# First loads of a decoder layer cut differently: activations in halves of 64 rows on both queues, first weights in three loads, four short warm-up products instead of seven

## The chip, the cores and the metric

The kernel runs on one core of one Trainium2 chip. The metric is device time in microseconds of one execution, the median of several. Profiles are single executions; their times count from the first instruction of the span.

TensorE multiplies matrices, VectorE and ScalarE work element by element, GpSimd does small side work. Transfers from main memory are issued on the queue of SyncE (SP) or of ScalarE (ACT), here called SP's queue and ScalarE's queue, and some on GpSimd's.

## The reference

One inference step of one decoder layer on 320 tokens: 256 of a prompt and 8 sequences of 8 sample tokens, with shared weights, model width 2048, all in 32-bit floats. Cut to what matters here:

```python
xn = rms_norm(x, g_mix)                      # x: 320 x 2048
z  = xn @ w_in                               # B, C, h, q, k, v and two gates
u  = c_gate * h_conv                         # short causal convolution, width 3
y_conv = (b_gate * short_conv(u)) @ w_conv_out
y_attn = window_attention(q, k, v, rel_bias, sinks) @ w_attn_out
h  = x + (sigmoid(gate_c) * y_conv + sigmoid(gate_a) * y_attn) @ w_o
hn = rms_norm(h, g_ffn)
h  = h + (silu(hn @ w_gate) * (hn @ w_up)) @ w_down
y  = rms_norm(h, g_final)
```

It returns the normalised output of both groups and the new key, value and convolution states.

## The kernel before

**Precision and layout.** Activations lie with features on the 128 partitions and the 320 tokens along the row: 16 chunks of 128 features. Each 32-bit factor is split into a high part, rounded to TensorE's 32-bit matmul type, and a low part, the remainder. A product of chunk k then takes three matmuls for each 128 output columns: high x times high w, low x times high w, high x times low w. For weights ScalarE makes the high part (`whi`) and VectorE the low part (`wlo`); for activations likewise (`xh_t`, `xl_t`), in `x_prep`, where for chunk 0 VectorE makes both. The norm's factor per token is applied later, so products can start on x times `g_mix`.

**Order of work.** The program is one long sequence of weight-driven products: first k and v (`kv_product`), then q, C, H, B, the gates, the attention between them, `w_o`, and the feed-forward part. Weights stream through four buffers of 512 KB (`wraw`). The order in which each engine takes its instructions comes from a scheduler of the language's layer: it places instructions by its own estimates, and adds the waits. A load that has to be counted takes one of eight counters in turn; when all eight are taken, the next load waits on its queue until the load that had that counter eight loads before has landed.

**The start.** This is all that the change touches.

- `xv` holds all activations and the small vectors. `x_load(i)` loads a stretch of its columns for all 128 partitions: `x_load(0)` the 16 columns of `g_mix` and chunk 0 (336 columns, 168 KB, line 290), `x_load(1)` chunk 1 (160 KB, on ScalarE's queue, line 294), later ones one or two chunks.
- `first_w` is the buffer of the weights of chunk 0 and chunk 1 for k and v, each 512 columns wide. Chunk 0 of it is loaded in two halves of 256 columns (128 KB each), the first on ScalarE's queue (line 292), the second on SP's (line 293). Chunk 1 (256 KB) follows on SP's queue from `load_kv` (line 331).
- ScalarE then loads its function table with a tiny square root (line 329), rounds chunk 0 in blocks of 128, 128 and 256 columns (line 337), and goes on chunk by chunk (line 129).
- While these loads are under way TensorE multiplies a constant by itself (lines 302 to 305): 15 warm-up products of 256 columns and 7 of 128, on bf16 ones that need no load. Their result is not used.
- `kv_product` (line 346, matmuls on line 372) runs over the 16 chunks, as tiles of 1, 1, 1, 1, 2, 2, 2, 2, 2, 2, with four blocks of 128 output columns: 12 matmuls of 320 columns a chunk. For chunk 0 the twelve are sorted by kind: four high-high, four with low x, four with low w.

Of the kernel before, what the change touches and what calls it, by code (L numbers as in the profile page):

```python
# [17 lines left out]
T = TP + NB * TS  # L18
# [8 lines left out]
P = 128  # L27
KC = D // P
CW = 256
# [7 lines left out]
VW = 16  # L37
# [15 lines left out]
def hybrid_layer(ctx: ExitStack, tc: tile.TileContext, a: dict, o: list):  # L53
    nc = tc.nc
    y_0, y_r, nk_p, nv_p, nk_s, nv_s, ncv = o

    w_in, w_kv, w_co, w_ao, w_o, w_g, w_u, w_d = (
        a[n] for n in ("w_in", "w_kv", "w_conv_out", "w_attn_out", "w_o", "w_gate", "w_up", "w_down")
    )
# [202 lines left out]
    xv = xp.tile([P, VX + 56], F32, name="xv")  # L262
# [23 lines left out]
    def x_load(i, eng=nc.sync):  # L286
        c0, c1 = (VW + sum(XB[:j]) * T if 0 < j < len(XB) else j and VX + 56 for j in (i, i + 1))
        return eng.dma_start(xv[:, c0:c1], a["x_v"][:, c0:c1])

    x_load(0)  # L290
    first_w = wp.tile([P, KT // 2, 2 * DKV], F32, tag="wraw", name="first_w", bufs=4)
    nc.scalar.dma_start(first_w[:, 0, 0:CW], w_kv[0, :, 0, 0:CW])
    nc.sync.dma_start(first_w[:, 0, CW:], w_kv[0, :, 0, CW:])
    behind = x_load(1, nc.scalar)
    first_root = st.tile([P, 1], F32, name="first_root")
# [5 lines left out]

    wm = ps_aux("wm")
    one = lambda n: nc.const_aps.tensor(1.0, [P, n], mybir.dt.bfloat16)
    for n in [CW] * 15 + [P] * 7:
        nc.tensor.matmul(wm[:, :n], one(P), one(n), start=True, stop=True)

    def x_prep(kc):
# [517 lines left out]
    for cp in range(4):  # L825
# [8 lines left out]
        for c in range(2):  # L834
# [13 lines left out]
            n = UL - 2  # L848
# [475 lines left out]
```

## Time and profile before

| | us |
|---|---|
| median of 3 runs | 1593.41 (1593.38 to 1593.64) |
| the profiled execution, its own time | 1593.85 |
| its span, first to last instruction | 1592.1 |
| TensorE busy in the span | 1583.2 |
| VectorE busy | 890.9 |
| ScalarE busy | 645.9 |
| first product of k and v starts | 4.43 |
| first product of chunk 1 starts | 7.20 |

The profile is read from its stages: a table that gives, for a stretch of the span, the busy time of each engine, the granted clock, the share of the 16 transfer engines in use and the rate in GB/s. The chain of waits goes back from the end to what released each step. In the timeline's rows the first two numbers are the start and the length in us; "idle before" in square brackets says how long the engine had stood still and what released it. PEld is TensorE's weight load, beside the matmuls. SPq and ACTq are instructions that issue transfers; their length is that of the issue, and the time to landing stands in the list of loads.

### The profile page before, as it was taken

The page shows a single profiled execution, that of the slowest core. Times are in us where ns is not written, and L with a number is a line of the kernel's source. Part 1 is how long each engine was busy: PE and PEld are TensorE (multiplying, and loading weights), DVE is VectorE, ACT ScalarE, POOL GpSimd, SP SyncE. Part 2 cuts the span into 40 slices and gives each one's busy share as a digit, 9 for nine tenths or more (in the row PEclk, how much of TensorE's full clock was granted, in tenths as well). Part 3 has the DMA queues.
Part 4 walks back from the last instruction along what each step waited for, and adds up shares of the span by engine and source line. Part 5 has one row for each costly group of instructions (what it writes and reads, how often), then busy time and mean ns, then how long its engine had stood idle before and what let it go on. Part 6 is the DMA issues. An engine that isn't in the chain of part 4 may idle for free.

```text
span 1592.1 us, 26453 instructions
## 1 busy us (share of the span) xinstructions
PE 1583.2 (99%) x10899; PEld 1547.1 (97%) x10899; DVE 890.9 (56%) x1314; ACT 645.9 (41%) x917; POOL 133.2 (8%) x213
## 2 busy tenths in 40 slices
PE   9999999999999999999999999999999999999998
PEld 9999999999999999999999999998888999999887
DVE  7879765445555445556555555553444455555556
ACT  7554443333333333344333333333333334444443
POOL 1414332000000003320000000000000000000021
PEclk9999999999999999999999999999999999999999
DMA  7757566544455544455554545555555454445663
GB/s 271 207 182 218 171 211 203 166 154 155 157 159 159 159 156 155 155 158 159 157 154 155 159 158 159 159 156 161 155 155 157 157 159 158 156 155 157 190 180 131
DMA packets 77648, 266.06 MB, mean 167 GB/s; under 512 B 9832, under 2 KB 13112, under 8 KB 77400
## 3 DMA queue, kind: packets, MB, share of 16 engines
q1 hardware_dynamic: 71736, 249.99, 50.2%
q0 software_dynamic: 5360, 13.84, 3.0%
q8 instruction: 85, 1.39, 0.4%
q10 hardware_dynamic: 432, 0.56, 0.1%
q14 instruction: 35, 0.29, 0.1%
HBM read 257.27 MB, written 9.04 MB: 167 GB/s over the span
## 4 chain that ended last, share of the span: by engine, by line
PE 99%; DMA 0%; DVE 0%; ACT 0%; issue 0%; SPq 0%; DVEq 0%
PE fu L186 19%; PE fg L186 19%; PE dn L997 9%; PE wo L186 7%; PE gc L186 7%; PE ga L186 7%; PE dn L1005 6%; PE C L186 3%; PE B L186 3%; PE H L186 3%; PE q L186 3%; PE ya L186 3%; PE yc L186 3%; PE dl L1001 2%; PE kv L372 2%; PE dn L1162 1%
## 5 line engine op out<-in xcount | busy, mean ns | idle before, releaser
L130 DVE TENSOR_TENSOR wlo<-wraw,whi 128x1024 fp32r<-128x1024 f32 (+1 forms) x460 | 563.1, 1225 | 564.5 <-ACT whi L129 453.4
L129 ACT ACTIVATE whi<-wraw 128x1024 fp32r<-128x1024 f32 (+1 forms) x460 | 485.5, 1056 | 722.0 <-PE fu L186 129.5
L186 PE MATMUL fu<-hh_t,whi 128*128 128x320 f32 x704 | 205.0, 301 | 0.0
L186 PE MATMUL fu<-hl_t,whi 128*128 128x320 f32 x704 | 205.0, 301 | 0.0
L186 PE MATMUL fg<-hh_t,whi 128*128 128x320 f32 x704 | 205.0, 301 | 0.0
L186 PE MATMUL fg<-hl_t,whi 128*128 128x320 f32 x704 | 205.0, 301 | 0.0
L186 PE MATMUL fu<-hh_t,wlo 128*128 128x320 f32 x704 | 158.8, 301 | 0.0
L186 PE MATMUL fg<-hh_t,wlo 128*128 128x320 f32 x704 | 158.8, 301 | 0.0
L997 PE MATMUL dn<-a_t,whi 128*128 128x512 f32 x640 | 155.2, 382 | 0.0
L186 PEld LDWEIGHTS fu<-hh_t,whi 128*128 128x128 f32 x704 | 131.7, 187 | 0.0
L186 PEld LDWEIGHTS fu<-hl_t,whi 128*128 128x128 f32 x704 | 131.7, 187 | 0.0
L186 PEld LDWEIGHTS fg<-hh_t,whi 128*128 128x128 f32 x704 | 131.7, 187 | 0.0
L186 PEld LDWEIGHTS fg<-hl_t,whi 128*128 128x128 f32 x704 | 131.7, 187 | 0.0
L997 PEld LDWEIGHTS dn<-a_t,whi 128*128 128x128 f32 x640 | 115.4, 187 | 16.5 <-issue 1.2
L186 PEld LDWEIGHTS fg<-hh_t,wlo 128*128 128x128 f32 x704 | 116.1, 187 | 0.0
L186 PEld LDWEIGHTS fu<-hh_t,wlo 128*128 128x128 f32 x704 | 116.1, 187 | 0.0
L1005 PEld LDWEIGHTS dn<-a_t,wlo 128*128 128x128 f32 x640 | 97.7, 188 | 6.9
L1005 PE MATMUL dn<-a_t,wlo 128*128 128x320 f32 x640 | 103.4, 301 | 0.0
L186 PE MATMUL gc<-xh_t,whi 128*128 128x320 f32 x256 | 74.5, 301 | 0.0
L186 PE MATMUL gc<-xl_t,whi 128*128 128x320 f32 x256 | 74.5, 301 | 0.0
L186 PE MATMUL ga<-xh_t,whi 128*128 128x320 f32 x256 | 74.5, 301 | 0.0
L186 PE MATMUL ga<-xl_t,whi 128*128 128x320 f32 x256 | 74.5, 301 | 0.0
(317 smaller groups left out, 2695.7 us busy)
## 6 DMA issues: line engine op xcount, KB each, us to landing
wraw<-in_w_in_dram SPq DMA_DIRECT2D x128, 512.0 KB, 3.9
wraw<-in_w_gate_dram SPq DMA_DIRECT2D x88, 512.0 KB, 3.8
wraw<-in_w_up_dram SPq DMA_DIRECT2D x88, 512.0 KB, 3.7
wraw<-in_w_down_dram SPq DMA_DIRECT2D x88, 512.0 KB, 3.7
wraw<-in_w_o_dram SPq DMA_DIRECT2D x32, 512.0 KB, 3.8
wraw<-in_w_conv_out_dram SPq DMA_DIRECT2D x16, 512.0 KB, 3.6
wraw<-in_w_attn_out_dram SPq DMA_DIRECT2D x16, 512.0 KB, 3.7
wraw<-in_w_kv_dram SPq DMA_DIRECT2D x6, 512.0 KB, 7.5
```

The source lines that it names most:

```text
L129: last["hi"] = nc.scalar.activation(hi, src, AF.Copy)
L130: last["lo"] = nc.vector.tensor_sub(lo, src, hi.bitcast(F32))
L186: last["mm"] = nc.tensor.matmul(turns(fives(ps[c][:, :T])), w[:, k, c * P:(c + 1) * P], turns(x(kc)), start=(kc == 0 and i == 0), stop=(kc ...
L372: last["mm"] = nc.tensor.matmul(turns(fives(ps[c][:, :T])), w[:, k, c * P:(c + 1) * P], turns(x(kc)), start=(kc == 0 and m == 0), stop=(kc ...
L997: nc.tensor.matmul(turns(placed(ps[c])), parts[k][0][:, cs], turns(a_move(k)), start=k == 0, stop=False)
L1001: nc.tensor.matmul(low, a_low(k), parts[k][0], start=k == 0, stop=k == nf - 1 and c0 < E0)
L1005: last["mm"] = nc.tensor.matmul(turns(placed(ps[c])[:, :, 0:JT]), parts[k][1][:, cs], turns(a_move(k)[:, :, 0:JT]), start=False, stop=k == ...
L1162: nc.tensor.matmul(turns(placed(ps[c])[:, :, JR:]), held[k][0][:, cs], turns(a_move(k)[:, :, JR:]), start=k == 0, stop=k == nf - 1,)
```

## The change

Three edits at the start of the program, and nothing else:

- `x_load(0)` becomes two loads of the same 336 columns: partitions 0 to 63 on SP's queue, 64 to 127 on ScalarE's.
- Chunk 0 of the first weights is loaded in three pieces: columns 0 to 127 on ScalarE's queue, 128 to 255 and 256 to 511 on SP's.
- The warm-up products of 128 columns are four, where they were seven.

```diff
-    x_load(0)
+    for rows, eng in ((slice(0, 64), nc.sync), (slice(64, P), nc.scalar)):
+        eng.dma_start(xv[rows, :VW + T], a["x_v"][rows, :VW + T])
     first_w = wp.tile([P, KT // 2, 2 * DKV], F32, tag="wraw", name="first_w", bufs=4)
-    nc.scalar.dma_start(first_w[:, 0, 0:CW], w_kv[0, :, 0, 0:CW])
+    nc.scalar.dma_start(first_w[:, 0, 0:P], w_kv[0, :, 0, 0:P])
+    nc.sync.dma_start(first_w[:, 0, P:CW], w_kv[0, :, 0, P:CW])
     nc.sync.dma_start(first_w[:, 0, CW:], w_kv[0, :, 0, CW:])
     behind = x_load(1, nc.scalar)
...
-    for n in [CW] * 15 + [P] * 7:
+    for n in [CW] * 15 + [P] * 4:
         nc.tensor.matmul(wm[:, :n], one(P), one(n), start=True, stop=True)
```

On SP's queue the program began, before the change, with these loads (a name in front of the arrow is where the load goes, behind it the source, then partitions x columns; `DMAHW0` and so on are the counters that a load waits for):

```order
L288 DMA xv<-in_x_v_dram 128x336
L293 DMA first_w<-in_w_kv_dram 128x256
L331 DMA first_w<-in_w_kv_dram 128x512
L288 DMA xv<-in_x_v_dram 128x320
L331 DMA wraw_191<-in_w_kv_dram 128x512
L288 DMA xv<-in_x_v_dram 128x320
L331 DMA wraw_191<-in_w_kv_dram 128x512 [waits DMAHW0_49]
L288 DMA xv<-in_x_v_dram 128x640 [waits DMAHW1_49]
```

With the change SP's queue begins so:

```order
L291 DMA xv<-in_x_v_dram 64x336
L294 DMA first_w<-in_w_kv_dram 128x128
L295 DMA first_w<-in_w_kv_dram 128x256
L333 DMA first_w<-in_w_kv_dram 128x512
L288 DMA xv<-in_x_v_dram 128x320
L333 DMA wraw_190<-in_w_kv_dram 128x512 [waits DMAHW0_49]
L288 DMA xv<-in_x_v_dram 128x320 [waits DMAHW1_49]
L333 DMA wraw_190<-in_w_kv_dram 128x512 [waits DMAHW2_49]
```

The load of weight chunk 1 (L331, now L333, 128x512 into `first_w`) moved from the third to the fourth place. The loads of weight chunk 2 and activation chunk 3, which waited for nothing, now wait for counters 0 and 1, which the two halves of the first activations hold.

On TensorE, the end of the warm-up products and the products of chunk 0, before:

```order
L305 MATMUL wm<-const-bfloat16-1.0 128x128
L372 MATMUL kv_143<-xh_t,whi_150 128x16x5x4 [waits DVE_49,Activation_49]
L372 MATMUL kv_144<-xh_t,whi_150 128x16x5x4 [waits Activation_49]
L372 MATMUL kv_145<-xh_t,whi_150 128x16x5x4 [waits Activation_49]
L372 MATMUL kv_146<-xh_t,whi_150 128x16x5x4
L372 MATMUL kv_143<-xl_t,whi_150 128x16x5x4 [waits DVE_49]
L372 MATMUL kv_144<-xl_t,whi_150 128x16x5x4
```

and with the change:

```order
L307 MATMUL wm<-const-bfloat16-1.0 128x128
L374 MATMUL kv_142<-xh_t,whi_149 128x16x5x4 [waits DVE_49,Activation_49]
L374 MATMUL kv_143<-xh_t,whi_149 128x16x5x4 [waits Activation_49]
L374 MATMUL kv_142<-xl_t,whi_149 128x16x5x4 [waits DVE_49]
L374 MATMUL kv_144<-xh_t,whi_149 128x16x5x4 [waits Activation_49]
L374 MATMUL kv_145<-xh_t,whi_149 128x16x5x4
L374 MATMUL kv_143<-xl_t,whi_149 128x16x5x4
```

The first product with the low activations (`xl_t`) moved from the fifth to the third place. ScalarE's queue issues three loads where it issued two: the second half of the first activations, the first 128 columns of weights, and activation chunk 1. Behind these places the order of instructions on every engine is the same in both programs.

## The prediction

> **What bounds the kernel now.** I read the page first, for the share of the engines.
>
> ```profile
> span 1592.1 us, 26453 instructions
> PE 1583.2 (99%) x10899; PEld 1547.1 (97%) x10899; DVE 890.9 (56%) x1314; ACT 645.9 (41%) x917; POOL 133.2 (8%) x213
> PE 99%; DMA 0%; DVE 0%; ACT 0%; issue 0%; SPq 0%; DVEq 0%
> ```
>
> TensorE is busy 1583.2 of 1592.1 us, so 8.9 us of the span are left for anything else. The table of stages (busy time and, behind it, the clock, the DMA share and the rate) tells where they lie.
>
> ```profile
> core 0: us, PE busy (x) PEld busy (x) DVE busy (x) ACT busy (x) POOL busy (x), PEclk, DMA share, GB/s
> 1.50:2.50 1.00, 1.00 (x7) 0.67 (x6) 0.00 (x0) 0.78 (x1) 0.78 (x3) 1.00 0.51 57
> 2.50:4.44 1.94, 1.82 (x16) 1.36 (x14) 0.66 (x2) 1.21 (x4) 0.00 (x0) 1.00 1.06 376
> 4.44:6.49 2.05, 2.05 (x12) 1.68 (x12) 1.59 (x3) 0.88 (x3) 0.00 (x0) 1.00 1.06 348
> 7.20:16.00 8.80, 8.80 (x62) 8.80 (x63) 8.57 (x16) 8.71 (x19) 2.70 (x6) 1.00 1.02 393
> 16.00:1584.80 1568.80, 1568.76 (x10806) 1534.08 (x10804) 877.44 (x1287) 631.98 (x888) 127.81 (x198) 1.00 0.53 165
> 1584.80:1592.10 7.30, 0.00 (x0) 0.00 (x0) 2.22 (x6) 1.71 (x4) 1.06 (x1) 0.67 0.60 229
> ```
>
> From 7.20 to 1584.8 us TensorE does not stop: 8.80 of 8.80 and 1568.76 of 1568.80. The tail of 7.3 us behind it contains no TensorE work. So whatever an edit does in the first microseconds reaches the end only by moving the moment 7.20, from which the unbroken run starts. The chain of waits over the first 10 us says what sets that moment (start, length, what):
>
> ```profile
> 0.80 0.39 SPq L288
> 1.24 0.42 SPq L293
> 1.70 4.79 DMA first_w<-in_w_kv_dram
> 6.52 0.64 ACT whi L129
> 7.20 2.83 PE kv L372 x18
> ```
>
> It is not the first activations and not the first weight chunk. It is the load of weight chunk 1 (I call it k1), third on SP's queue, issued at 1.70 and landed at 6.49; then ScalarE's rounding of it, 0.64 us, and TensorE at 7.20. Before that, TensorE has worked off chunk 0:
>
> ```profile
> 3.74 0.55 DVE L309 TENSOR_SCALAR xh_t<-xv 128x320 fp32r<-128x320 f32 x1 [2.42 <-DMA xv<-in_x_v_dram]
> 3.94 0.94 ACT L337 ACTIVATE whi<-first_w 128x128 fp32r<-128x128 f32 x3 [0.72 <-DMA first_w<-in_w_kv_dram]
> 4.43 1.05 PE L372 MATMUL kv<-xh_t,whi 128*128 128x320 f32 x4
> 5.32 0.72 PE L372 MATMUL kv<-xl_t,whi 128*128 128x320 f32 x4
> 5.88 0.72 PE L372 MATMUL kv<-xh_t,wlo 128*128 128x320 f32 x4
> 7.20 0.42 PE L372 MATMUL kv<-xh_t,whi 128*128 128x320 f32 x1 [0.60 <-ACT whi L129]
> ```
>
> Its twelve products start between 4.43 and 6.30. Those of a full-rate group are (0.72 - 0.30) / 3 = 0.14 us apart (0.30 is what one takes), so the thirteenth could start at 6.44; it starts at 7.20. This 0.76 us is all that chunk 0's timing has to spare, and all that an earlier k1 alone could give.
>
> **Is k1 late because the transfers are saturated?** Ahead of and with k1 lie 168 + 128 + 128 + 160 + 256 = 840 KB, 0.86 MB (the sizes are in the next rows: first activations, first weights in two parts, second activations on ScalarE's queue, k1). By the table of stages 57 + 1.94 x 376 + 2.05 x 348 = 1500 KB (in thousands of bytes) had moved by 6.49; 0.86 MB had moved by about 4.65. So 0.64 MB of later transfers moved before k1's last piece came in, and that last piece is about 1.8 us behind the mean rate. A load counts as landed when its last part has landed; one laggard among the parts decides here, not the order of issue.
>
> **The change part by part.** The issue rows (start, length) and the time to landing of the same loads:
>
> ```profile
> 0.79 0.41 ACTq L292 DMA_DIRECT2D first_w<-in_w_kv_dram  x1
> 1.24 0.45 ACTq L288 DMA_DIRECT2D xv<-in_x_v_dram  x1
> 1.72 1.28 ACT L329 ACT_TABLE_LOAD   x1 [1.72 <-PEq L1304]
> 2.66 0.43 SPq L331 DMA_DIRECT2D wraw<-in_w_kv_dram  x1
> 3.93 0.33 SPq L331 DMA_DIRECT2D wraw<-in_w_kv_dram  x1
> 6.51 0.33 SPq L331 DMA_DIRECT2D wraw<-in_w_kv_dram  x1
> 7.87 0.62 ACT L129 ACTIVATE whi<-wraw 128x512 fp32r<-128x512 f32 x1
> wraw<-in_w_kv_dram SPq DMA_DIRECT2D x2, 256.0 KB, 4.8
> first_w<-in_w_kv_dram SPq DMA_DIRECT2D x1, 256.0 KB, 4.8
> xv<-in_x_v_dram SPq DMA_DIRECT2D x1, 168.0 KB, 2.9
> first_w<-in_w_kv_dram ACTq DMA_DIRECT2D x1, 128.0 KB, 3.1
> first_w<-in_w_kv_dram SPq DMA_DIRECT2D x1, 128.0 KB, 3.2
> xv<-in_x_v_dram ACTq DMA_DIRECT2D x1, 160.0 KB, 3.4
> ```
>
> *Activations in halves.* The first 168 KB become 84 KB on each queue, at 0.80 and 0.79. Both must land before VectorE's L309 can start. If each half took half of the 2.9 us that lie between issue and landing, it would land 1.45 us earlier; but the stage 1.50:2.50 shows 57 GB/s against 376 in the next, with the same queues filled: the start of motion costs most of it. From 2.50 on, 168 KB at 376 GB/s take 0.46 us, and before they shared that rate with 128 KB of weights, 0.81 us together; so between nothing and 0.35 us earlier, and I take 0.2: the halves are joined by 128 KB of weights right behind, as before.
>
> The Trainium skill, page "DMA: Bandwidth & Descriptors", section "Rules for kernel authors", says of two transfers to disjoint partition halves that one need not bother, as both spread over the same engines. By that rule this term would be 0, by the rows 0.2 us earlier; the DMA share of 1.06 with two queues filled agrees that they share one capacity.
>
> *First weights in three loads.* The first block of 128 columns goes out second on ScalarE's queue, at about 1.24 instead of 0.79, the second block second on SP's. If 3.1 us to landing holds from the issue, the first block lands at 4.34 instead of 3.9, 0.44 later; if what counts is the bytes, 64 + 64 KB are in with the same bytes ahead and come at the old time. ScalarE also issues one load more ahead of its table load, which thus ends near 3.45 instead of 3.0 (1.72 + 1.28), still half a microsecond ahead of the weights at 3.94. I take +0.1 for the first product, at most +0.44, against the 0.2 us gained on the activations, which both must be there: the first product stands between 4.3 and 4.9. Even 4.9 puts the thirteenth at 6.9, still ahead of 7.20. That cover is the 0.76 us above; without it the worst case would cost those 0.44 us in full.
>
> *Everything behind on SP's queue.* Two loads more are counted in all, one of them on SP, so k1 goes out fourth on SP, one issue (1.70 - 1.24 = 0.46) later, at 2.16. Here lies the price that the trace can't settle. Two ends: loads of 256 KB took 4.8 us from issue to landing, the one issued at 1.70 and the two behind it alike; if that holds, k1 lands at 6.96 and the run starts 0.46 later. If the backlog holds, it costs nothing: the weights' third part landed at 1.24 + 3.2 = 4.44, so at 2.16 SP's transfers still had 2 us of other bytes ahead of k1, and the total is unchanged. The rate row of 376 GB/s with a share of 1.06 is nearer to the second: 0. On the other side, a new cut of the rows may hit no laggard; then k1 lands before 5.7 and the run starts at 6.44: -0.76. I take the middle of +0.46 and -0.76, -0.15.
>
> *The loads behind k1.* They now wait for a landing two loads further on: in the order of the change the third chunk's load waits on the first half of the activations. It went out at 2.66 with no wait; it goes out when that half has landed, 3.4 to 3.7, about 0.9 later. That it is a real wait is seen in the row at 3.93, which goes when the first weights landed (ScalarE starts on them at 3.94), and that at 6.51, right behind k1's landing at 6.49. What is queued behind it on SP is the next activations and the fourth chunk. The third chunk landed at 2.66 + 4.8 = 7.5 and is rounded at 7.87; TensorE wants it at 7.20 + 12 x 0.14 = 8.88, so with 0.62 us for the rounding the landing may slip to 8.2, that is by 0.7. A slip of 0.9 in full would cost 0.2; since bytes and not issues are the limit, I take 0.
>
> *Three warm-up products fewer, and one product moved.* Chunk 0's third product is now one on the low activations (ready at 4.87, 4.32 + 0.55, by the trace's next VectorE step), in place of one on the third weight block (ready at 3.94 + 0.94 = 4.88): 0.
>
> ```profile
> 0.83 2.72 PE L305 MATMUL wm<-const-bfloat16-1.0 128*128 128x256 bf16 x12 [0.83 <-PEq L1304]
> 3.52 0.80 PE L305 MATMUL wm<-const-bfloat16-1.0 128*128 128x256 bf16 x9
> 4.32 0.55 DVE L312 SCALAR_TENSOR_TENSOR xl_t<-xv,xh_t 128x320 fp32r<-128x320 f32 x1
> L305 PE MATMUL wm<-const-bfloat16-1.0 128*128 128x256 bf16 x15 | 3.1, 389 | 0.8 <-PEq L1304 0.8
> L305 PE MATMUL wm<-const-bfloat16-1.0 128*128 128x128 bf16 x7 | 0.6, 221 | 0.0
> ```
>
> The first 12 are (2.72 - 0.39) / 11 = 0.21 us apart, 1.2 columns a ns; the last nine, two wide and seven short, bring 1280 columns in 0.80 - 0.22 us, 2.2 a ns. So the clock rose at about 3.5 us, though the column of granted clock says 1.00 throughout. Three short ones at 2.2 columns a ns are 0.17 us: the warm-ups end at 4.15 instead of 4.32. The activations are ready at 3.74 + 0.55 = 4.29, so the warm-ups were hardly in the way; the gap ahead of the first product grows to about 0.3 us. Price on the end: 0.
>
> **The sum.** In the profiled execution: run start 7.20, minus 0.15, plus 1577.6 us of unbroken products and 7.3 us of tail: 1591.95 of span, and 1.75 around it (1593.85 measured against 1592.1), 1593.7. That execution lies 0.44 above the median of the runs; on the median, 1593.41 - 0.15 = 1593.3 us.
>
> **The rivals.**
>
> *A, the laggard goes.* k1 lands by 5.7, the run starts as soon as chunk 0 is done. For it: 0.64 MB overtook k1's last piece, which is no steady state. Against it: both other 256 KB loads took 4.8 us too. Price -0.76, up to -0.96 with the activations 0.2 earlier: 1592.5 to 1592.7. VectorE and ScalarE, at 8.57 and 8.71 of 8.80 us, leave little room to feed a faster run than that.
>
> *B, slower: issue counts.* k1 lands 4.8 us after its later issue: +0.46, 1593.9; if the third chunk slips too, 1594.1. For it the equal 4.8 us of three loads; against it the backlog. It decides from the point where k1 lands after 6.49.
>
> *C, the late clock.* The clock is raised later than at 3.5 us in other executions. The warm-ups then run at 0.21 and 0.105 us, seven short ones end at 0.83 + 3.15 + 0.74 = 4.7, four at 4.4; chunk 0 at half rate lasts 3.4 us, so TensorE and not k1 sets the run's start, and 0.3 us are saved: 1593.1. The trace holds one execution only, with the rise at 3.5. The Trainium skill, page "TensorE: Matmul & The Clock Gate", section "What you observe" and what follows it, has the window free-running and the count of slow products varying from run to run, which is this rival; no row here shows a second phase.
>
> *D, the clock falls back.* The longer gap of 0.3 us lets TensorE's clock stay or return to half. Chunk 0 then takes 1.68 us more, its end moves from 6.44 to 8.12, 0.92 past 7.20; each further chunk costs another 1.68. Against it: TensorE already stood still for 0.60 us ahead of 7.20, and the products after it keep the full rate. With chunk 0 and 1 slow: 1596.0.
>
> *E, nothing moves:* k1 and its laggard land as before; 1593.4. It is inside the forecast's own spread.
>
> **How the numbers follow.** Forecast with E, -0.4 to +0.3 around it: 0.60. A 0.15, B 0.18, C 0.04, D 0.03. What a measurement of this kernel can tell from no change is about 0.2%, 3.2 us. No case but a long D reaches it: even A is 0.06%. Faster by more: 0.01; slower by more: 0.02 (D, and small unknowns); within: 0.97. The range takes in A at its lower end (1592.4) and B at its upper with the 0.44 us by which one execution already differed from the others: 1592.4 to 1594.3.
>
> **What would show it.** In the changed kernel's chain the load of chunk 1 still stands ahead of the unbroken run, issued near 2.16, and TensorE's idle time ahead of it between 0 and 1 us. The first product starts at 4.3 to 4.9. The third chunk's load is issued after 3.3. The warm-ups end near 4.15, and from the second chunk on products are 0.14 us apart. I am wrong in the mechanism if TensorE stops anywhere after its second chunk, if the products of chunk 0 or 1 are 0.28 apart, or if the run starts before 6.2 or after 8.

## The result and the profile after

The changed kernel takes 1595.70 us (median of 22 runs, 1594.58 to 1597.05), the kernel before 1593.55 us (1592.95 to 1594.08). The ratio is 1.0013 with a 95% interval of 1.0007 to 1.0019: slower by 2.15 us. That lies inside 0.2% as forecast, but the interval is clear of 1, and the time is outside the predicted range of 1592.4 to 1594.3. Two runs at several thousand us, one of before here and one of e8 below, were disturbed and are left out of every range.

The profiled execution of the changed kernel took 1595.98 us with a span of 1594.2. Its table of stages, with the same columns as the one of before:

```profile
1.50:2.50 1.00, 1.00 (x7) 0.69 (x6) 0.00 (x0) 0.00 (x0) 0.77 (x3) 1.00 0.29 65
2.50:4.44 1.94, 1.94 (x12) 1.43 (x10) 0.70 (x2) 1.49 (x2) 0.00 (x0) 1.00 0.78 195
4.44:6.49 2.05, 1.24 (x6) 1.06 (x5) 0.97 (x2) 0.82 (x3) 0.00 (x0) 1.00 1.00 345
16.00:1584.80 1568.80, 1568.80 (x10811) 1534.79 (x10811) 878.39 (x1287) 633.54 (x892) 130.25 (x201) 1.00 0.53 165
1586.50:1594.20 7.70, 0.00 (x0) 0.00 (x0) 2.22 (x6) 1.70 (x4) 1.07 (x1) 0.71 0.58 218
```

The row from 16.00 us is as before: TensorE does not stop behind the start. The second row and the last are not.

Between 2.50 and 4.44 us the transfers moved 195 GB/s; before, in the same stage, 376. That is (376 - 195) x 1.94 = 350 KB less, close to 1 us of transfer at the old rate. By 2.50 us as much had moved as before (65 KB, 57 before), so the loss lies within this stage. The DMA share fell less than the rate, from 1.06 to 0.78: the transfer engines stood still more, and also moved less while they were busy (195 / 0.78 = 250 GB/s against 376 / 1.06 = 355).

The last row is the tail, from TensorE's last product to the end. It takes 7.7 us where it took 7.3. Both kernels end with SyncE waiting on the eight transfer counters, one after the other in a fixed order. The change counts two loads more, so every later transfer has a counter two further on. Before, the last output write had the counter that is asked last but one; now it has the one that is asked first, and seven waits of about 0.06 us each follow behind its landing. SyncE's waits for the output, first before, then with the change (us in total, times, longest):

```profile
SPq L1312 <- DMA out_dram<-ya: 1.8, 3, 0.8
SPq L1314 <- DMA out_dram<-ya: 2.3, 1, 2.3
```

That write lands 6.4 us behind TensorE's last product in both. All seven profiles with two loads more (the change, its two repeats, e1, e5, e7 and e8 below) have a tail of 7.75 to 7.77 us, the seven others one of 7.28 to 7.36. So about 0.43 us of the loss arise at the end of the program and have nothing to do with late data or the clock. No experiment was made for this path alone; the profiles show it.

The chain of waits over the first 10 us:

```profile
0.80 0.58 ACTq L291
1.42 3.63 DMA first_w<-in_w_kv_dram
5.07 0.32 ACT whi L339
5.43 4.68 PE kv L374 x18
```

It now runs through the first weight block, second on ScalarE's queue, and no longer through weight chunk 1. The rows of the timeline behind it:

```profile
0.80 0.58 SPq L291 DMA_DIRECT2D xv<-in_x_v_dram  x1
0.83 3.79 PE L307 MATMUL wm<-const-bfloat16-1.0 128*128 128x256 bf16 x19 [0.83 <-PEq L1306]
1.42 0.86 ACTq L293 DMA_DIRECT2D first_w<-in_w_kv_dram  x1
1.44 0.56 SPq L294 DMA_DIRECT2D first_w<-in_w_kv_dram  x1
5.43 0.90 PE L374 MATMUL kv<-xh_t,whi 128*128 128x320 f32 x2 [0.81 <-ACT whi L339]
7.32 0.61 ACT L129 ACTIVATE whi<-first_w 128x512 fp32r<-128x512 f32 x1
7.73 1.27 PE L374 MATMUL kv<-xh_t,wlo 128*128 128x320 f32 x4
8.79 0.47 PE L374 MATMUL kv<-xh_t,whi 128*128 128x320 f32 x1
9.33 0.36 PE L374 MATMUL kv<-xh_t,whi 128*128 128x320 f32 x1
9.52 0.31 PE L374 MATMUL kv<-xl_t,whi 128*128 128x320 f32 x1
9.67 0.30 PE L374 MATMUL kv<-xh_t,whi 128*128 128x320 f32 x1
```

Two things are to be seen. The loads of 64 rows were issued in 0.58 us, where 128 rows had taken 0.39; the load behind on ScalarE's queue took 0.86 us to issue (0.41 before), and landed at 1.42 + 3.63 = 5.05. So the first product starts at 5.43, 1.0 us later than before, after TensorE has stood still for 0.81 us. And its clock is still low: four products of chunk 0 take 1.27 us, (1.27 - 0.47) / 3 = 0.27 us apart, and the spacing falls to 0.14 only at about 9.4 us. Before, that fall came near 3.5 us, in the warm-up products.

Chunk 1 starts at 8.79, at 7.20 before. Its weights were rounded by 7.93 (the row at 7.32: ScalarE came to them late, behind the second activations, which landed at 2.31 + 4.4 = 6.7 where they had landed at 1.24 + 3.4 = 4.6). With a raised clock chunk 1 could so have started at about 8.0, an estimate; a2 below does at 8.03. Of the 1.59 us some 0.8 are then late data and 0.8 the low clock. The 1.59 us, 0.11 in the run of products behind it and 0.43 in the tail are together the 2.13 us between the two profiled executions.

### The profile page after: what moved, and what is told of

It is laid out like the page before. It is cut to its first block, busy times and chain, and to the rows that moved or that the text cites. A ratio compares the mean times of both kernels' runs of the same rounds, so it can differ in the third digit from the quotient of the medians.

```text
span 1594.2 us, 26451 instructions
## 1 busy us (share of the span) xinstructions
PE 1584.8 (99%) x10896; PEld 1549.0 (97%) x10896; DVE 891.7 (56%) x1314; ACT 645.8 (41%) x917; POOL 134.0 (8%) x213
## 4 chain that ended last, share of the span: by engine, by line
PE 99%; DMA 0%; DVE 0%; ACT 0%; issue 0%; DVEq 0%; ACTq 0%
PE fu L186 19%; PE fg L186 19%; PE dn L999 9%; PE wo L186 7%; PE ga L186 7%; PE gc L186 7%; PE dn L1007 6%; PE C L186 3%; PE B L186 3%; PE H L186 3%; PE q L186 3%; PE ya L186 3%; PE yc L186 3%; PE dl L1003 2%; PE kv L374 2%; PE dn L1164 1%
## 5 line engine op out<-in xcount | busy, mean ns | idle before, releaser
L186 PE MATMUL wo<-m_h,whi 128*128 128x320 f32 x256 | 74.5, 301 | 0.0
```

Of the source, the lines that this page charges most:

```text
L186: last["mm"] = nc.tensor.matmul(turns(fives(ps[c][:, :T])), w[:, k, c * P:(c + 1) * P], turns(x(kc)), start=(kc == 0 and i == 0), stop=(kc ...
```

## The experiments

Two theories stood against each other, with variants. **Late weights and a late clock:** the cut loads bring the first operands late, TensorE pauses, and because of the pause its clock rises later. **Warm-ups:** the three missing products alone delay the clock. A third holds that all of it is late data and the clock plays no part. The runs came in three groups, each timed beside the kernel before (1593.52, 1593.63 and 1593.56 us).

| kernel | loads | warm-ups | us, median (range) | ratio, 95% |
|---|---|---|---|---|
| before | as before | 15 wide + 7 short | 1593.55 (1592.95 to 1594.08) | |
| the change | both cuts | 15 + 4 | 1595.70 (1594.58 to 1597.05) | 1.0013 [1.0007, 1.0019] |
| e2 | as before | 15 + 4 | 1593.46 (1592.88 to 1593.91) | 1.0000 [0.9991, 1.0008] |
| e6 | as before | 12 + 0 | 1594.89 (1593.08 to 1595.30) | 1.0008 [0.9999, 1.0017] |
| e4 | weights cut | 15 + 7 | 1593.92 (1593.72 to 1595.73) | 1.0003 [0.9994, 1.0012] |
| e3 | activations in row halves | 15 + 7 | 1594.83 (1593.97 to 1596.17) | 1.0010 [1.0001, 1.0019] |
| e9 | activations in column halves | 15 + 7 | 1594.59 (1594.00 to 1595.09) | 1.0006 [0.9997, 1.0015] |
| e1 | both cuts | 15 + 7 | 1595.15 (1594.84 to 1596.23) | 1.0011 [1.0002, 1.0020] |
| e5 | both cuts | 15 + 16 | 1595.39 (1594.78 to 1595.96) | 1.0011 [1.0003, 1.0020] |
| e7 | both cuts, column halves | 15 + 4 | 1594.53 (1594.38 to 1596.47) | 1.0010 [1.0001, 1.0018] |
| e8 | both cuts, weights first | 15 + 4 | 1594.47 (1594.08 to 1594.62) | 1.0005 [0.9996, 1.0014] |

### The warm-ups alone

```diff
 # e2, against the kernel before
-    for n in [CW] * 15 + [P] * 7:
+    for n in [CW] * 15 + [P] * 4:
```

> The kernel before with four short warm-up products in place of seven, loads untouched. Late-weights theory: first product at 4.4, clock up by 3.5 to 7 us, 1593.5, no change. Warm-up theory: the whole loss of the change appears, 1595 to 1596.

Measured: 1593.46 us, ratio 1.0000. Four short warm-ups cost nothing where the loads are as before. The warm-up theory falls. This execution's TensorE rows also show something about the kernel before:

```profile
5.82 0.72 PE L372 MATMUL kv<-xh_t,wlo 128*128 128x320 f32 x4
6.46 0.41 PE L372 MATMUL kv<-xh_t,whi 128*128 128x320 f32 x1
```

Chunk 1 starts at 6.46 with no wait, where the profile of before had 7.20 with 0.60 us of waiting. The loads and the code ahead of chunk 1 are the same, so the late weight chunk 1, from which the prediction took all its cover, is not there in every execution.

```diff
 # e1, against the change
-    for n in [CW] * 15 + [P] * 4:
+    for n in [CW] * 15 + [P] * 7:
```

> The change with seven short warm-up products again, both cuts of the loads kept. Late-weights theory (the first weight block, now behind half of the activations on ScalarE's queue, lands near 5.0 us instead of 3.9; TensorE stands still and its clock rises later): the block still lands near 5.0 and the first product still starts near 5.4, so at least 0.8 us over before stay (1594.3 or more); the pause ahead of the product is 0.3 us shorter, which may bring the clock's rise forward. Warm-up theory (the three missing products alone delay the clock): back to 1593.5.

Measured: 1595.15 us, 1.0011. Most of the loss stays with the warm-ups restored. Nine of its 11 runs lie at 1594.84 to 1595.22 and two at 1596.2; of the change's 22 runs, 12 lie above 1595.5. By these counts the three short products move how often an execution falls in the upper group, and not where the groups lie. One expectation missed: the first 128 columns did not land near 5.0, and the first product started at 4.46. This time the load with the long issue stood on SP's queue, and what came late were the second and third parts of the weights:

```profile
1.40 0.60 ACTq L293 DMA_DIRECT2D first_w<-in_w_kv_dram  x1
1.45 0.81 SPq L294 DMA_DIRECT2D first_w<-in_w_kv_dram  x1
5.35 0.41 PE L374 MATMUL kv<-xh_t,whi 128*128 128x320 f32 x1 [0.51 <-ACT whi L339]
6.68 0.55 PE L374 MATMUL kv<-xh_t,whi 128*128 128x320 f32 x2 [0.92 <-ACT whi L339]
8.19 0.30 PE L374 MATMUL kv<-xh_t,whi 128*128 128x320 f32 x1
```

Which queue pays changes; chunk 1 starts at 8.19 all the same.

### Each cut of the loads alone

```diff
 # e3, against the kernel before
-    x_load(0)
+    for rows, eng in ((slice(0, 64), nc.sync), (slice(64, P), nc.scalar)):
+        eng.dma_start(xv[rows, :VW + T], a["x_v"][rows, :VW + T])
```

> Only the first activations in halves on both queues; first weights in two loads, seven short warm-ups, as before. Late-weights theory: the first 256 columns of weights are second on ScalarE's queue, land at 4.6 to 5.2 and the first product starts at 5.0 to 5.5; 1594.3 to 1595.7. If the three-part cut of the weights were the cause: 1593.5.

Measured: 1594.83 us, 1.0010. The halves alone cost 1.3 us at the median. ScalarE's issue rows and TensorE's first product:

```profile
0.80 0.58 ACTq L291 DMA_DIRECT2D xv<-in_x_v_dram  x1
1.41 0.86 ACTq L293 DMA_DIRECT2D first_w<-in_w_kv_dram  x1
5.68 1.44 PE L373 MATMUL kv<-xh_t,whi 128*128 128x320 f32 x4 [0.74 <-ACT whi L338]
7.98 1.27 PE L373 MATMUL kv<-xh_t,wlo 128*128 128x320 f32 x4
```

The same two marks as in the change: 0.58 and 0.86 us of issue, a first product at 5.68, and a low clock (1.27 us for four). This execution took 1596.02.

```diff
 # e4, against the kernel before; ScalarE's order of steps held as before
-    nc.scalar.dma_start(first_w[:, 0, 0:CW], w_kv[0, :, 0, 0:CW])
+    nc.scalar.dma_start(first_w[:, 0, 0:P], w_kv[0, :, 0, 0:P])
+    nc.sync.dma_start(first_w[:, 0, P:CW], w_kv[0, :, 0, P:CW])
...
             if i == 0:
-                x_prep(1)
+                with after(last["hi"]):
+                    x_prep(1)
```

> Only the first weights in three loads (activations whole on SP's queue, seven short warm-ups; the order of ScalarE's steps held as before). Late-weights theory: the first 128 columns are first on ScalarE's queue and land by 3.9, chunk 0's product starts at 4.4, weight chunk 1 goes out 0.46 later on SP's queue; 1593.3 to 1593.9. If the cut of the weights were the cause: the first block's landing moves to 4.5 or later, 1594.5 or more.

Measured: 1593.92 us, 0.02 above the range of the late-weights theory; the ratio is 1.0003 with an interval that holds 1. The first block landed by 3.7 and the first product started at 4.35, as expected; the third part of the weights came late, and TensorE waited for it:

```profile
2.50:4.44 1.94, 1.94 (x16) 1.52 (x15) 0.89 (x2) 1.21 (x4) 0.00 (x0) 1.00 0.95 271
5.99 0.55 PE L374 MATMUL kv<-xh_t,whi 128*128 128x320 f32 x2 [1.11 <-ACT whi L338]
7.50 0.30 PE L374 MATMUL kv<-xh_t,whi 128*128 128x320 f32 x1
```

The rate of the early stage fell to 271 GB/s from this cut alone. In e3 it was 286, with both cuts 195 to 231 in the change, its two repeats and e1, against 376 before, 372 in e2 and 378 in e6. Every kernel with untouched loads has the high rate and every kernel with cut loads a lower one.

### The clock alone

```diff
 # e6, against the kernel before
-    for n in [CW] * 15 + [P] * 7:
+    for n in [CW] * 12:
```

> The kernel before with 12 wide warm-up products and no short ones, loads untouched: the warm-ups end near 3.4 us at half clock and TensorE pauses 1 us ahead of its first product at 4.4. Clock theory: the data comes as before, but the clock rises between 7 and 10 us in most executions, chunk 0's products are 0.27 us apart, median 1594.0 to 1594.6. Loads-only theory: 1593.5, since the warm-ups compute nothing.

Measured: 1594.89 us; nine of the 11 runs lie at 1594.45 to 1595.30, above every one of the 33 runs of before beside it (highest 1594.06), and two at 1593.08 and 1593.35. The interval of the ratio, 0.9999 to 1.0017, just holds 1. The profiled execution was one of the two quick ones: products at full rate, and chunk 1 at 6.44.

```profile
5.87 0.73 PE L372 MATMUL kv<-xh_t,wlo 128*128 128x320 f32 x4
6.44 0.30 PE L372 MATMUL kv<-xh_t,whi 128*128 128x320 f32 x1
```

> The kernel before with 12 wide warm-ups (e6_gap12) once more. Clock theory: with about 9 chances in 11 an execution near 1594.9 in which chunk 0's products are 0.27 us apart and the clock turns after 7 us, with the loads landing as before (first weights 3.9, first product 4.4). Loads-only theory: a late load in it.

Measured: 1595.34 us in this one execution of the same kernel.

```profile
2.50:4.44 1.94, 1.05 (x5) 0.44 (x3) 0.56 (x2) 1.11 (x4) 0.00 (x0) 1.00 1.05 378
0.83 2.72 PE L305 MATMUL wm<-const-bfloat16-1.0 128*128 128x256 bf16 x12 [0.83 <-PEq L1304]
4.53 0.87 PE L372 MATMUL kv<-xh_t,whi 128*128 128x320 f32 x2 [0.98 <-DVE xh_t L309]
6.80 1.27 PE L372 MATMUL kv<-xh_t,wlo 128*128 128x320 f32 x4
7.87 0.47 PE L372 MATMUL kv<-xh_t,whi 128*128 128x320 f32 x1
9.41 0.30 PE L372 MATMUL kv<-xh_t,whi 128*128 128x320 f32 x1
```

The loads came at the full 378 GB/s and the first product at 4.53, nearly as before. But TensorE had paused 0.98 us, its products stayed 0.27 us apart until about 9.3 us, and the execution cost 2.3 us more than the quick one of the same kernel. Here no load was late, and the loads-only theory falls: with a pause of 1 us ahead of the first product, and nothing else changed, the clock can stay low to above 9 us. It need not: the quick execution of e6 had a pause of 0.87 us at the same place.

```diff
 # e5, against the change
-    for n in [CW] * 15 + [P] * 4:
+    for n in [CW] * 15 + [P] * 16:
```

> The change with 16 short warm-up products instead of 4, loads as changed. At half clock the warm-ups then reach to about 5.75 us, past the first product's 5.43. Clock theory (a pause of 1 us ahead of the first product makes TensorE's clock rise one evaluation of about 3.4 us later in about half of the executions): the upper half of the change's times goes away, all near 1594.6 to 1595.4, median about 1595.0, and products of chunk 0 are 0.14 us apart or the clock is up by 7 us. Loads-only theory (all 2.1 us are late data): median stays at 1595.7 with times up to 1597.

Measured: 1595.39 us, 1594.78 to 1595.96. The times above 1596, seven of the change's 22, are gone, as the clock theory has it; the median fell by 0.3 us where 0.7 was expected. The extra products stand in the way themselves (first product at 5.60 instead of 4.46 in e1, at the same landing of the first block). The bridge repays little of what it removes.

### The change twice more

> The changed kernel once more, one execution with its profile. Clock theory: the time goes with the moment at which TensorE's products turn from 0.27 to 0.14 us apart: below 1595.2 if that is before 6 us, above 1595.5 if it is at 8.5 to 10 us. Loads-only theory: the time goes with the landing of the first weights, whatever the clock does.

> As a1_again: the changed kernel, one more execution, to pair another time with another moment of the clock's rise.

Measured: 1594.63 and 1595.22 us. Of a1:

```profile
0.83 3.50 PE L307 MATMUL wm<-const-bfloat16-1.0 128*128 128x256 bf16 x19 [0.83 <-PEq L1306]
5.15 0.61 PE L374 MATMUL kv<-xh_t,whi 128*128 128x320 f32 x2 [0.82 <-ACT whi L339]
7.16 0.74 PE L374 MATMUL kv<-xh_t,wlo 128*128 128x320 f32 x4
7.74 0.30 PE L374 MATMUL kv<-xh_t,whi 128*128 128x320 f32 x1
```

and of a2:

```profile
5.17 0.61 PE L374 MATMUL kv<-xh_t,whi 128*128 128x320 f32 x2 [0.55 <-ACT whi L339]
7.06 0.74 PE L374 MATMUL kv<-xh_t,wlo 128*128 128x320 f32 x4
8.03 0.41 PE L374 MATMUL kv<-xh_t,whi 128*128 128x320 f32 x1 [0.23 <-ACT whi L129]
```

In both the products are at full rate (0.74 us for four). In a1 the 19 warm-ups take 3.50 us instead of 3.79, so the clock rose while they ran; it then stayed up through a pause of 0.82 us. In a2 they take 3.79 us, as in the first profile, so there the clock rose only behind them, during the pause of 0.55 us. With nearly the same late first product (5.15 and 5.17, against 5.43) these executions are 1.4 and 0.8 us quicker than the first profiled one. With the clock up the change still costs about 1.1 to 1.7 us against the median before: 0.43 of it is the tail, the rest late data, with chunk 1 at 7.74 and 8.03. The time of a2 is 0.02 above what the clock theory expected for so early a rise.

Each trace also keeps a record of the stretch in which the full clock was granted. The views print 1.00 ahead of its first entry, which is why their column shows no rise.

| profile | TensorE's pause ahead of the first product | full clock from | for |
|---|---|---|---|
| before | 4.31 to 4.43 | 3.46 | 1583.784 |
| a1 | 4.33 to 5.15 | 3.87 | 1583.784 |
| e6 | 3.55 to 4.42 | 4.13 | 1583.784 |
| a2 | 4.62 to 5.17 | 4.82 | 1583.784 |
| g1 | 3.55 to 4.53 | 9.33 | 1580.371 |
| the change | 4.62 to 5.43 | 9.42 | 1580.371 |
| e3 | 4.94 to 5.68 | 10.03 | 1580.371 |

The other seven profiles have a start between 3.58 and 5.54 and 1583.784 us. The two lengths differ by 3.413 us. The three late executions thus passed a moment 3.41 us earlier, at 5.91, 6.01 and 6.61, without a rise, and in each the whole pause lies in the 3.41 us ahead of that moment. In a1 the pause follows the rise; in e6 and a2 the rise falls into the pause. So a raised clock survives the pause, as it does in e4, e7 and e9, which stood still for 1.11, 1.31 and 1.71 us behind the rise; and a pause ahead of the rise can cost one step of 3.41 us. Whether it does depends on where these moments lie, and they differ from execution to execution; this agrees with the two groups of times of e6 and of the change. How much of a pause is too much is not shown: before also had no work ahead of 0.83 us, 0.78 of the 3.41 us ahead of its rise.

### Where the halves' price comes from

```diff
 # e7, against the change
-    for rows, eng in ((slice(0, 64), nc.sync), (slice(64, P), nc.scalar)):
-        eng.dma_start(xv[rows, :VW + T], a["x_v"][rows, :VW + T])
+    for c0, c1, eng in ((0, VW + T // 2 - 8, nc.sync), (VW + T // 2 - 8, VW + T, nc.scalar)):
+        eng.dma_start(xv[:, c0:c1], a["x_v"][:, c0:c1])
```

> The change with the first activations halved by columns (128 rows x 168 columns on each queue) instead of by rows. If 64 rows are what makes the issue long (0.58 us against 0.39, and up to 0.86 for the load behind it): issues of 0.4 to 0.45 us, first movement before 2.0 us, first weight block lands by 4.5, 1594.0 to 1594.6. If it is only the second place on ScalarE's queue: issues as in the change, landing near 5, 1595 to 1596.

Measured: 1594.53 us; seven runs at 1594.38 to 1594.68, four at 1595.8 to 1596.5.

```profile
0.79 0.41 ACTq L291 DMA_DIRECT2D xv<-in_x_v_dram  x1
1.23 0.46 ACTq L293 DMA_DIRECT2D first_w<-in_w_kv_dram  x1
2.50:4.44 1.94, 1.94 (x13) 1.48 (x11) 1.00 (x2) 1.69 (x4) 0.00 (x0) 1.00 0.90 201
6.42 0.55 PE L374 MATMUL kv<-xh_t,whi 128*128 128x320 f32 x2 [1.31 <-ACT whi L339]
```

With 128 rows the issues are short again and the first block is in time (first product at 4.38): the long issues belong to the loads of 64 rows. Yet the early rate is no better, 201 GB/s, and now the third part of the weights is late, with a wait of 1.31 us. The time is where the 64-rows reading expected it, 1.2 us below the change at the median, but for another reason than issues alone, and still 0.9 us above before, 0.4 of them the tail.

```diff
 # e9, against the kernel before
-    x_load(0)
+    for c0, c1, eng in ((0, VW + T // 2 - 8, nc.sync), (VW + T // 2 - 8, VW + T, nc.scalar)):
+        eng.dma_start(xv[:, c0:c1], a["x_v"][:, c0:c1])
```

> The kernel before with only the first activations halved, by columns: 128 rows x 168 columns on each queue; weights in two loads, seven short warm-ups. If the row halves' long issues (0.58 and 0.86) are what makes e3_halves_only slow: issues near 0.4, first weights landed by 4.2, 1593.4 to 1594.0. If any second load ahead of the weights on ScalarE's queue does it: weights after 4.7, 1594.5 or more.

Measured: 1594.59 us, outside what the first theory expected (1594.0 at most), though the first weights landed at 4.2 as it said. In the profiled execution, 1595.09, the second activations on ScalarE's queue took 5.60 us to land, and chunk 1 waited for them behind chunk 0:

```profile
1.72 5.60 DMA xv<-in_x_v_dram
8.54 0.41 PE L373 MATMUL kv<-xh_t,whi 128*128 128x320 f32 x1 [1.71 <-ACT whi L129]
```

So the long issue is not the whole of the price: at the median the column halves cost 1.0 us, the row halves 1.3, a difference that the intervals don't tell from none. In each of the profiles of e3, e4, e7 and e9 some load among the first comes late, not always the same: the first weights, their third part (twice), the second activations.

```diff
 # e8, against the change: first weight block ahead of the half on ScalarE's queue
-    for rows, eng in ((slice(0, 64), nc.sync), (slice(64, P), nc.scalar)):
-        eng.dma_start(xv[rows, :VW + T], a["x_v"][rows, :VW + T])
     first_w = wp.tile([P, KT // 2, 2 * DKV], F32, tag="wraw", name="first_w", bufs=4)
     nc.scalar.dma_start(first_w[:, 0, 0:P], w_kv[0, :, 0, 0:P])
+    for rows, eng in ((slice(0, 64), nc.sync), (slice(64, P), nc.scalar)):
+        eng.dma_start(xv[rows, :VW + T], a["x_v"][rows, :VW + T])
```

> The change with the first weight block ahead of the half of the activations on ScalarE's queue. Queue-place theory: the block lands by 3.9 again, the activations' second half near 4.0, first product at 4.6 to 4.8, 1593.7 to 1594.3. If a load of 64 rows is dear wherever it stands: it is still issued in 0.58 us or more, the load behind it takes longer still, and the late load is another (second activations or weights on SP's queue): 1594.5 or more.

Measured: 1594.47 us, between what the two theories expected.

```profile
0.79 0.39 ACTq L291 DMA_DIRECT2D first_w<-in_w_kv_dram  x1
2.50:4.44 1.94, 1.70 (x12) 1.18 (x10) 0.52 (x1) 1.81 (x4) 0.00 (x0) 1.00 0.97 255
4.61 0.53 PE L374 MATMUL kv<-xh_t,whi 128*128 128x320 f32 x2 [0.41 <-DVE xh_t L311]
```

The first block, ahead on its queue, is issued in 0.39 us and in time; the first product starts at 4.61 and waits for the activations. The early rate is 255 GB/s, still well below 376. The place on the queue changes which load is late; the lower rate stays, and so does the tail of 7.76 us, half of the 0.9 us that this version is above before.

No version was quicker than the kernel before; e2 is not told from it.

## Why the prediction was wrong

**The frame held for the products, not for the tail.** Behind the start TensorE does not stop, and its last product moves with the start of chunk 1. Between them lie 1577.57 us in the profile of before, 1577.68 in the change, and 1577.3 to 1577.7 in every other profile in which the clock was up by then, but for e8, where products came late twice more, at 8.80 and 12.53 us (1578.05). With a low clock at chunk 1 it is 1577.95 in e3 and 1578.41 in g1. But "whatever an edit does in the first microseconds reaches the end only by moving the moment 7.20" failed: the tail, 7.3 us in the sum, took 7.77. The prediction saw that "Two loads more are counted in all" and followed it to the loads behind k1 only, not to the waits on the same counters at the end.

**Its own signs spoke against it.** The chain no longer runs through the load of chunk 1, products of chunk 0 and the first ones of chunk 1 are 0.27 us apart, and the unbroken run starts at 8.79, past the 8 that it named.

**The step that failed first: the rate.** The prediction said of the loads that "if what counts is the bytes, 64 + 64 KB are in with the same bytes ahead and come at the old time", and of weight chunk 1 that the backlog at 376 GB/s made the price 0. The bytes are the same, the rate is not: 195 instead of 376 GB/s in the stage that matters. The term "+0.1 for the first product, at most +0.44" measured +1.0 in the profiled execution and +0.7 in the two repeats, and "the first product stands between 4.3 and 4.9" became 5.15 to 5.43. Issue times were taken over from loads of 128 rows (0.39 and 0.41); 64 rows took 0.58 and the load behind up to 0.86.

**The second: the cover.** "This 0.76 us is all that chunk 0's timing has to spare" came from one execution with a late chunk 1. In e2 and e6 chunk 1 starts at 6.46 and 6.44, with nothing to spare, so any delay of chunk 0 goes to the end. Rival A, priced at -0.76, was no rival to be won by the change; it is how the kernel before runs in some of its executions, and probably part of its spread from 1592.95 to 1594.08.

**The third: the clock.** Rival D had the mechanism in part, with 0.03: a longer pause keeps the clock low. It was sized with a pause of 0.3 us (the pause was 0.8) and argued away because TensorE "already stood still for 0.60 us ahead of 7.20" at full rate. That pause came after the rise, and a1 shows that a raised clock lives through such a pause; it says nothing on a pause before the rise. D's price for a slow chunk 0 and 1, 1596.0, meets the 1595.98 of the profiled execution by luck: it has no late data and no longer tail in it. Rival C, the late clock that saves 0.3 us, was seen nowhere: in the change and in a2 the clock was still low when the warm-ups ended, and the first product waited for its weights all the same.

**Rival B** had the sign right: issue times count. Its price of 0.46, at weight chunk 1, missed the place; what was late was first_w's first block, in other executions its second or third.

**What held.** The warm-ups' own cost was put at 0: e2 measured no difference. The change in the order of chunk 0's products was put at 0, and nothing spoke against it. The third chunk's load went out at 3.69, after 3.3 as predicted, and did not reach the end. The rule cited on partition halves (not worth it) points the right way, but the term drawn from it, 0, and the one drawn from the rows, 0.2 us earlier, both left out a loss.

**By size:** of the 2.15 us, the cut loads with seven warm-ups make 1.6 (e1), 0.4 of it the tail. Alone the row halves cost 1.3 (e3) and the weights' cut 0.4 (e4, not told from 0); each counts one load more, and neither has the longer tail (7.28 and 7.33 us). The remaining 0.55 us go with the shorter warm-ups only where the loads are late (0 in e2): 12 of 22 executions above 1595.5, instead of two in 11. These are differences of medians, each uncertain by 1 to 1.5 us by the intervals.

## What to carry to other kernels

Cutting the first loads smaller, to spread them over two queues, can lower the rate at which they all arrive; read the early stage's GB/s and the issue lengths, and don't carry a rate or an issue time from loads of 128 rows to loads of 64. Take a cover of a few tenths from several executions, never from one. Ask of a pause of TensorE in the first 10 us whether its clock has risen yet, by the spacing of equal products: ahead of the rise a pause of 0.7 to 1 us can cost 3.4 us more at half clock, behind it pauses of 0.8 to 1.7 us left the clock up. And where a change adds or takes away counted loads, compare the tails too: here two loads more at the start cost 0.43 us at the end.

## What the runs showed of the hardware

- A load of 64 rows x 336 columns was issued in 0.55 to 0.60 us, one of 128 rows x 336 in 0.39, one of 128 x 168 in 0.39 to 0.41. Where two loads of 64 rows were issued at the same moment, the next load on one of the two queues took 0.77 to 0.86 us to issue (the change, a1, a2, e3 on ScalarE's queue, e1 and e5 on SP's), and it landed at 4.8 to 5.3 us, 3.4 to 3.9 us after its issue. Why, the records don't tell.
- The early rate fell with every cut: 372 to 378 GB/s untouched, 271 to 286 with one cut, 195 to 255 with both, at a DMA share of 0.78 to 0.97 against 1.05 to 1.06. At 2.50 us as much or more had moved with the cuts as without (65 to 131 KB from 1.50 us on, against 51 to 64), so the loss is not a later start of movement. Which of the loads stand in each other's way was not separated, and why the rate falls stays open.
- The full clock was granted from 3.46 to 5.54 us in eleven profiles and from 9.33 to 10.03 in three (g1, the change, e3), each with a pause of 0.74 to 0.98 us ahead of it. The late ones have 3.413 us less of it (1580.371 against 1583.784). The profile's column of granted clock said 1.00 throughout; the products' spacing (0.27 and 0.14 us) and the record of the clock showed the rise. The Trainium skill, page "TensorE: Matmul & The Clock Gate", section "What's actually happening", has a free-running activity window of 3413 ns. The trace agrees with it: by the 3.413 us, and by moments that differ from execution to execution.
- The waits on the transfer counters at the end of the program took about 0.06 us each once their counter was reached. The tail is 7.75 to 7.77 us where the last output write has the counter asked first, and 7.28 to 7.36 us where it has the last or the last but one.
